# A down product set between the halves of the next expert's up product, expert weights read in longer runs, and a Hyena product taken last

## The chip, the cores and the metric

The kernel runs on one core of a Trainium2 chip (trn2). A core has a matrix engine (TensorE, PE in the profile; its weight loads are PEld), a vector engine (VectorE, DVE), an activation engine (ScalarE, ACT), GpSimd (POOL) and SyncE (SP), each with its own in-order queue, and 16 DMA engines that all queues share. The metric is the device time of one execution in microseconds; the time of record is the median of several runs.

## The reference, cut to what matters

The reference runs two blocks one after the other: a first block of two layers (an MLA attention layer and a Hyena layer with long convolutions), and a second block with sliding-window attention, an HGRN2 recurrence and a mixture of 32 experts with top-2 routing over 1024 tokens of width 1024. The change touches the projection of the Hyena layer and the experts:

```python
def hyena_seq(t, w_in, conv_w, conv_b, spec, bias, w_out):
    u, gate = jnp.split(t @ w_in, [(HY_ORDER + 1) * HY_WIDTH], axis=-1)   # t: 1024 x 1024, w_in: 1024 x 4096
    u = depthwise_conv(u, conv_w, conv_b)
    ...

    def expert_block(args):
        xb, e = args
        h = jax.nn.silu(xb @ w_gate[e]) * (xb @ w_up[e])   # w_gate, w_up: 1024 x 512
        return h @ w_down[e]                               # w_down: 512 x 1024
    y_blocks = lax.map(expert_block, (x_blocks, blk_e))
```

## The kernel before

Every large product is computed in a split form: each float32 operand is written as hi + lo (hilo, lines 162 to 165: ACT copies to hi, VectorE subtracts to get lo), and mm3 (lines 185 to 188) takes three matmuls, hi hi, hi lo and lo hi, into one PSUM tile. A planner (the tile scheduler, with a simulated timeline) lays down the order of each engine's instructions and gives out buffers when the program is built; the order of the statements is its priority.

**Hyena projection.** Lines 1015 to 1056 go over four column blocks c of 256 and, in each, over four chunks of the 4096 output columns: part 0 and part 1 (v and the first gate), the second gate, and the silu gate. Each chunk loads its weights (wchunk, lines 917 to 942) and projects (proj, lines 957 to 985); the first three also run a short convolution (convs and taps), and parts 0 and 1 are then transposed (line 1028). The projection is a fast matrix multiplication in the manner of Strassen and Winograd: seven products of half size in place of eight, on sums of weight blocks (s1 = x21 + x22, s2 = s1 - x11, s3 = x11 - x21, s4 = x12 - s2, made by GpSimd in total from two buffers in turn) and on sums of inputs (t1 to t4). Each product takes one PSUM bank out of a pool of five (ps3), is 12 matmuls of 512 columns and is then added into the result d by VectorE (add); the first, x11, is copied by ACT (line 971). In the chunks with a convolution d is a tile u, of which there are two for each chunk's two halves, so that a new chunk's first copy waits for the taps of the chunk before. The order of the products is x11, x12, s2, s3, s4, s1, x22. The weight tiles of each kind have one buffer (pool hywo), written by split for the next chunk when the product has read them. Only the first chunk has a hook, mid, and runs in two cuts of 256 columns.

**Experts.** Each of the 32 experts is a generator, expert (lines 1930 to 1992). It gathers up to 112 token rows by an indirect DMA on GpSimd's queue (xg), transposes them (line 1955) and splits them to xh and xl; then come the gate product (two weight tiles), the up product (two tiles), h = silu(gate) * up, the transposes of h (line 1977) with their split to hh and hl, the down product (two tiles, one for each half of the output columns), ACT's scaling to y (line 1989) and an accumulating indirect DMA of y to the output (line 1990). A weight tile is 1 MiB, [128, 4, 512]; load (lines 1935 to 1947) takes one of the raw buffers (slot_of: 11, later 8), issues one DMA on SP's queue and splits it into one of five hi and lo pairs. Of gate and up, partition p holds rows k * 128 + p, so that a tile has four runs of 2 KB in each partition; of down, a tile is 512 of 1024 columns of such rows, again runs of 2 KB. The driver (lines 2009 to 2014) steps through the generators with next: in iteration e it takes the gather of expert e+1, the first half of gate(e), the transposes of h(e-1), the second half of gate(e), down(e-1) and up(e). Two loads wait for marks (GATE, n = 9 and 10), and y comes from another pool when n has reached 62.

## Time and profile before

| | us |
|---|---|
| median of 3 runs | 3277.11 (3276.27 to 3277.31) |
| the profiled execution | 3279.27 |
| its span, first to last instruction | 3277.2 |
| TensorE busy in the span | 3089.8 (94%) |
| VectorE busy | 2467.8 (75%) |
| ACT busy | 1499.8 (46%) |
| GpSimd busy | 647.2 (20%) |
| mean granted TensorE clock | 0.979 |

Rows of the profile give times from the start of the span. A busy TensorE is not TensorE at its peak, since matmuls are pipelined and overlap; the spacing of their starts tells more than their durations. Idle time in brackets stands ahead of an instruction, with what ended it. The share of a DMA queue is the time of its packets as a share of 16 engines' time in the window.

### The profile page before, as it was taken

Reading aid. Unit: us, or ns where it says so; the run is one execution under the profiler, and the core shown is the slowest. Engines: PE = TensorE matmul, PEld = TensorE weight load, DVE = VectorE, ACT = ScalarE, POOL = GpSimd, SP = SyncE. Lnnn points to the kernel's source line nnn. Section 1 sums busy time; section 2 is a strip of 40 time slices with the busy share of each in tenths; the row PEclk is TensorE's granted clock in tenths of the full one; section 3 lists DMA queues with packets and bytes.
Section 4 is the critical chain, followed back from the end, with each engine's and each line's share of the span. In section 5 each row is a group of like instructions: output and inputs, shape, how many; then the busy total and the mean of one; then the engine's idle time right before and its main releaser. Section 6 shows DMA issues by size and latency. Waiting matters only on the chain. (4 is left out here: it accounts for less than half of the span.)

```text
span 3277.2 us, 49862 instructions
## 1 busy us (share of the span) xinstructions
PE 3089.8 (94%) x18178; PEld 2699.5 (82%) x18178; DVE 2467.8 (75%) x5292; ACT 1499.8 (46%) x2624; POOL 647.2 (20%) x523
## 2 busy tenths in 40 slices
PE   7899999999999899999999899999999989999997
PEld 3789888898987777889997799888878978777775
DVE  4985347888768888789897776576746689888886
ACT  2432234454543444421114345454523368777775
POOL 2651000000001434445750000000000024441110
PEclk9999999999999899999999999999999989999999
DMA  7562231331224222263426311312344689999996
GB/s 244 177 193 76 75 98 56 106 99 51 81 79 128 70 98 103 71 231 107 144 86 196 118 41 56 115 58 75 102 151 159 212 294 346 340 344 342 345 343 214
DMA packets 368879, 510.16 MB, mean 156 GB/s; under 512 B 59002, under 2 KB 211234, under 8 KB 368632
## 3 DMA queue, kind: packets, MB, share of 16 engines
q1 hardware_dynamic: 355464, 474.15, 43.8%
q0 software_dynamic: 13168, 32.81, 3.7%
q8 instruction: 144, 2.36, 0.3%
q14 instruction: 103, 0.84, 0.1%
HBM read 426.82 MB, written 92.61 MB: 158 GB/s over the span
## 5 line engine op out<-in xcount | busy, mean ns | idle before, releaser
L165 DVE TENSOR_TENSOR ewl<-ewr,ewh 128x1024 fp32r<-128x1024 f32 (+1 forms) x394 | 449.0, 1195 | 71.1 <-ACT ewh L164 70.1
L164 ACT ACTIVATE ewh<-ewr 128x1024 fp32r<-128x1024 f32 (+1 forms) x394 | 381.3, 1033 | 55.2 <-DMA ewr<-in_w_gate_experts_dram 20.4
L187 PE MATMUL ez<-ewl,xh 128*128 128x512 f32 x512 | 203.2, 397 | 5.9 <-DVE ewl L165 5.8
L186 PE MATMUL ez<-ewh,xh 128*128 128x512 f32 x512 | 201.3, 395 | 7.7 <-ACT ewh L164 7.7
L188 PE MATMUL ez<-ewh,xl 128*128 128x512 f32 x512 | 199.6, 390 | 0.0
L893 POOL TENSOR_TENSOR sd0h<-Yh,T 128x512 f32<-128x512 f32 x2 | 5.6, 2809 | 775.2 <-issue 769.9
L187 PE MATMUL cz<-cTl,w5h 128*128 128x512 f32 x384 | 152.7, 398 | 0.0
L186 PE MATMUL cz<-cTh,w5h 128*128 128x512 f32 x384 | 152.6, 399 | 0.0
L188 PE MATMUL cz<-cTh,w5l 128*128 128x512 f32 x384 | 152.1, 399 | 0.0
L164 ACT ACTIVATE pth<-tr 128x512 fp32r<-128x512 f32 x160 | 92.0, 594 | 130.1 <-PE tr L764 129.5
L747 DVE TENSOR_SCALAR_CACHE_REDUCE pr<-s 128x512 f32<-128x512 f32 (+1 forms) x192 | 109.2, 595 | 17.2 <-PE tr L764 11.2
L186 PEld LDWEIGHTS ez<-ewh,xh 128*128 128x128 f32 x512 | 96.4, 188 | 30.2 <-ACT ewh L164 10.4
L187 PEld LDWEIGHTS ez<-ewl,xh 128*128 128x128 f32 x512 | 96.4, 188 | 28.3 <-DVE ewl L165 9.1
L165 DVE TENSOR_TENSOR ptl<-tr,pth 128x512 fp32r<-128x512 f32 x160 | 107.4, 684 | 14.5 <-ACT pth L164 13.9
L186 PE MATMUL dz<-ewh,hh 128*128 128x512 f32 x256 | 101.2, 399 | 12.4 <-ACT hh L164 8.7
L188 PEld LDWEIGHTS ez<-ewh,xl 128*128 128x128 f32 x512 | 96.2, 188 | 19.0
L1990 POOL DMA_INDIRECT out_dram<-y,idx x32 | 75.6, 2364 | 170.9 <-ACT y L1989 129.7
L186 PE MATMUL oz<-owh,oh 128*128 128x512 f32 x256 | 102.4, 404 | 5.9 <-ACT owh L164 3.9
L751 ACT ACTIVATE pr<-pr,mx 128x1280 f32<-128x1280 f32 x64 | 87.3, 1364 | 41.1 <-DVE mx L750 40.6
L188 PE MATMUL oz<-owh,ol 128*128 128x512 f32 x256 | 100.8, 398 | 2.1 <-DVE ol L165 2.1
L187 PE MATMUL oz<-owl,oh 128*128 128x512 f32 x256 | 101.9, 399 | 0.0
L187 PE MATMUL dz<-ewl,hh 128*128 128x512 f32 x256 | 100.0, 391 | 0.2 <-DVE ewl L165 0.2
(758 smaller groups left out, 10827.1 us busy)
## 6 DMA issues: line engine op xcount, KB each, us to landing
ewr<-in_w_up_experts_dram SPq DMA_DIRECT2D x64, 1024.0 KB
ewr<-in_w_gate_experts_dram SPq DMA_DIRECT2D x64, 1024.0 KB
ewr<-in_w_down_experts_dram SPq DMA_DIRECT2D x64, 1024.0 KB
spec<-so SPq DMA_DIRECT2D x64, 256.0 KB
adaw<-in_ada_w_dram SPq DMA_DIRECT2D x64, 256.0 KB
hwr<-in_hy_w_in_dram SPq DMA_DIRECT2D x64, 256.0 KB
K<-spec SPq DMA_DIRECT2D x64, 256.0 KB
w5r<-in_w_in_dram SPq DMA_DIRECT2D x60, 256.0 KB
```

The lines of the kernel that those rows point to most:

```text
L164: S.activation(hi, x, AF.Copy)
L165: V.tensor_tensor(lo, x, rd(hi), ALU.subtract)
L186: T.matmul(ps, lh, rh, start=first, stop=False)
L187: T.matmul(ps, lh, rl, start=False, stop=False)
L188: return T.matmul(ps, ll, rh, start=False, stop=last)
L747: V.tensor_scalar(pr[:, k0:k0 + n], z[:, :n], 1.0, None, ALU.mult, ALU.max, accum_out=mx[:, c:c + 1])
L751: S.activation(pr, pr, AF.Exp, scale=SC, bias=mx[:, 3:4], accum_out=sm)
L893: G.tensor_tensor(t4, rd(yh[:, 4:, tk]), t2, ALU.subtract)
L1990: G.indirect_dma_start(out=out_d, out_offset=bass.IndirectOffsetOnAxis(ap=ix[:BR], axis=0), in_=y[:BR], in_offset=None, bounds_check=1023, ...
```

## The change

In proj, the s4 product moves from fifth to last place (in the cut that starts at column 256 it stays first, and in the first cut of the chunk with the hook it stays where it was). In expert, three things change. The weights are read so that partition p holds neighbouring rows, p * 8 + k for gate and up and p * 4 + k for down, and a tile is then one run of 8 KB in each partition; the transposes of xg and h read columns with a step of 8 and of 4 elements to match. A down tile is now two rows of all 1024 columns in each partition, so both output halves accumulate at once in two PSUM tiles over both weight tiles, and both loads stand ahead of the first matmul. The up product yields between its halves, and the driver takes one step more, so that iteration e is: gather of e+1, first half of gate(e), transposes of h(e-1), second half of gate(e), first half of up(e), down(e-1), second half of up(e).

```diff
--- before.py
+++ after.py
@@ -974,15 +974,15 @@
                 z22 = product("s4", "y22") if r.start else None
                 add(0, 1, (1, 0), product("s2", "t2"))
                 add(1, 1, (0, 1), product("s3", "t3"))
-                z22 = z22 or product("s4", "y22")
                 if mid and not r.start:
+                    z22 = product("s4", "y22")
                     with tc.issue_after(pe[0].ins):
                         mid()
                 z = product("s1", "t1")
                 add(1, 0, (1, 1), product("x22", "t4"))
                 add(1, 1, (1, 1), z)
                 add(0, 1, (0, 1), z)
-                add(0, 1, (0, 1), z22)
+                add(0, 1, (0, 1), z22 or product("s4", "y22"))
 
         def convs(wt, ct, mid=None):
 
@@ -1930,7 +1930,9 @@
     def expert(px, pw, praw, ps, pst, xg, ix, wt, e, static=True):
 
         def src(w):
-            return (w[e] if static else w[bass.ds(e, 1)].rearrange("o d f -> (o d) f")).rearrange("(k p) f -> p k f", p=P)
+
+            w = (w[e] if static else w[bass.ds(e, 1)].rearrange("o d f -> (o d) f")).rearrange("(p k) f -> p (k f)", p=P)
+            return w[:, :2048], w[:, 2048:]
 
         def load(w):
             n = n_raw[0]
@@ -1938,7 +1940,7 @@
             raw = slot_of(n).tile([P, 4, 512], F32, tag="ewr", name="ewr")
             if n in GATE:
                 V.tensor_copy(raw[:, 0, :1], GATE[n])
-            SY.dma_start(raw, w)
+            SY.dma_start(raw.rearrange("p k f -> p (k f)"), w)
             hi = pw[n % 5].tile([P, 4, 512], F32R, tag="ewh", name="ewh")
             lo = pw[n % 5].tile([P, 4, 512], F32R, tag="ewl", name="ewl")
             m = 1 if n < 5 else 2
@@ -1949,21 +1951,22 @@
                              bounds_check=1023, oob_is_err=False)
         xh = px.tile([P, 8, P], F32R, tag="xh", name="xh")
         xl = px.tile([P, 8, P], F32R, tag="xl", name="xl")
+        xk = xg.rearrange("t (p k) -> t k p", k=8)
         for k4 in range(2):
             z = pst.tile([P, 4, P], F32, tag="tr", name="tr")
             for k in range(4):
-                T.transpose(z[:, k], xg[:, (k4 * 4 + k) * P:(k4 * 4 + k + 1) * P], ident)
+                T.transpose(z[:, k], xk[:, k4 * 4 + k], ident)
             hilo(xh[:, k4 * 4:k4 * 4 + 4], xl[:, k4 * 4:k4 * 4 + 4], z)
         yield
         zz = []
         for w in (wg, wu):
             z = ps.tile([P, 512], F32, tag="mm", name="ez")
             for k4 in range(2):
-                wh, wl = load(src(w)[:, k4 * 4:k4 * 4 + 4])
+                wh, wl = load(src(w)[k4])
                 for k in range(4):
                     kk = k4 * 4 + k
                     mm3(z, xh[:, kk], xl[:, kk], wh[:, k], wl[:, k], kk == 0, kk == 7)
-                if w is wg:
+                if w is wg or k4 == 0:
                     yield
             zz.append(z)
         h = px.tile([P, 512], F32, tag="h", name="h", bufs=1)
@@ -1973,20 +1976,22 @@
         hh = px.tile([P, 4, P], F32R, tag="hh", name="hh", bufs=1)
         hl = px.tile([P, 4, P], F32R, tag="hl", name="hl", bufs=1)
         z = pst.tile([P, 4, P], F32, tag="tr", name="tr")
+        hk = h.rearrange("t (p k) -> t k p", k=4)
         for k in range(4):
-            T.transpose(z[:, k], h[:, k * P:(k + 1) * P], ident)
+            T.transpose(z[:, k], hk[:, k], ident)
         hilo(hh, hl, z)
         yield
         if n_raw[0] < 62:
             y = px.tile([P, 1024], F32, tag="y", name="y")
         else:
             y = praw[0].tile([P, 4, 512], F32, tag="ewr", name="y")[:, :2].rearrange("p a c -> p (a c)")
-        for c in range(2):
-            z = ps.tile([P, 512], F32, tag="mm", name="dz")
-            wh, wl = load(src(wd)[:, :, c * 512:(c + 1) * 512])
-            for k in range(4):
-                mm3(z, hh[:, k], hl[:, k], wh[:, k], wl[:, k], k == 0, k == 3)
-            S.activation(y[:BR, c * 512:(c + 1) * 512], z[:BR], AF.Copy, scale=wt[:BR])
+        zz = [ps.tile([P, 512], F32, tag="mm", name="dz") for _ in range(2)]
+        ws = [load(w) for w in src(wd)]
+        for c, k in ((0, 0), (1, 0), (0, 1), (1, 1), (0, 2), (0, 3), (1, 2), (1, 3)):
+            wh, wl = (x[:, k % 2 * 2 + c] for x in ws[k // 2])
+            mm3(zz[c], hh[:, k], hl[:, k], wh, wl, k == 0, k == 3)
+            if k == 3:
+                S.activation(y[:BR, c * 512:(c + 1) * 512], zz[c][:BR], AF.Copy, scale=wt[:BR])
         G.indirect_dma_start(out=out_d, out_offset=bass.IndirectOffsetOnAxis(ap=ix[:BR], axis=0), in_=y[:BR], in_offset=None,
                              bounds_check=1023, oob_is_err=False, compute_op=ALU.add)
         yield
@@ -2010,7 +2015,7 @@
     next(blocks[0])
     for e in range(33):
         cur, prev = [blocks[e]] if e < 32 else [], [blocks[e - 1]] if e else []
-        for b in blocks[e + 1:e + 2] + cur + prev + cur + (prev + cur if e < 31 else cur + prev):
+        for b in blocks[e + 1:e + 2] + cur + prev + cur + cur + (prev + cur if e < 31 else cur + prev):
             next(b)
         if 2 <= e < 18:
 
```

## Rows read from the trace of the kernel before

**Rows 1.** The page: busy time of TensorE, and DMA share in 40 slices

```profile
PE 3089.8 (94%) x18178; PEld 2699.5 (82%) x18178; DVE 2467.8 (75%) x5292; ACT 1499.8 (46%) x2624; POOL 647.2 (20%) x523
DMA  7562231331224222263426311312344689999996
```

**Rows 2.** Hyena chunks: stretch, us, busy PE PEld DVE ACT POOL, clock, DMA share, GB/s

```profile
1119.66:1144.88 25.22, 23.14 (x101) 18.64 (x100) 20.65 (x24) 11.60 (x22) 10.34 (x9) 0.93 0.35 125
1183.64:1205.01 21.37, 21.37 (x101) 17.73 (x100) 16.65 (x22) 10.17 (x21) 6.82 (x7) 1.00 0.15 49
1205.01:1233.27 28.26, 24.09 (x101) 19.29 (x100) 21.40 (x24) 11.93 (x23) 11.71 (x8) 0.88 0.31 112
...
1381.98:1410.45 28.47, 24.30 (x101) 19.50 (x100) 21.40 (x24) 12.04 (x23) 11.70 (x8) 0.88 0.06 19
```

**Rows 3.** Timeline of TensorE, 1216 to 1223: start, us, instruction [idle before, releaser]

```profile
1216.14 0.50 PE L186 MATMUL uz<-Y22h,s4h 128*128 128x512 f32 x1
...
1221.04 0.79 PE L188 MATMUL uz<-Y22h,s4l 128*128 128x512 f32 x1 [4.17 <-DVE s4l L165]
1221.64 0.63 PE L186 MATMUL uz<-Y22h,s4h 128*128 128x512 f32 x1
1222.06 0.63 PE L187 MATMUL uz<-Y22l,s4h 128*128 128x512 f32 x1
```

**Rows 4.** Timeline of ACT, the copy of line 971

```profile
1223.43 0.60 ACT L971 ACTIVATE u<-uz 128x512 f32<-128x512 f32 x1
```

**Rows 5.** Timeline of VectorE, 1202 to 1224

```profile
1202.40 0.69 DVE L165 TENSOR_TENSOR s1l<-ws,s1h 128x512 fp32r<-128x512 f32 x1 [2.37 <-ACT s1h L164]
1205.21 0.69 DVE L968 TENSOR_TENSOR u<-u,uz 128x512 f32<-128x512 f32 x1 [2.12 <-PE uz L188]
...
1207.96 1.27 DVE L968 TENSOR_TENSOR u<-u,uz 128x512 f32<-128x512 f32 x2
...
1220.31 0.68 DVE L165 TENSOR_TENSOR s4l<-ws,s4h 128x512 fp32r<-128x512 f32 x1
1220.91 2.43 DVE L1006 SCALAR_TENSOR_TENSOR y<-u,cw,y 128x512 f32<-128x512 f32 x2
```

**Rows 6.** The columns of rows 2, two stretches of the experts

```profile
2700.00:2800.00 100.00, 99.73 (x475) 82.68 (x475) 92.94 (x93) 84.76 (x103) 44.88 (x26) 1.00 1.02 347
2800.00:3250.00 450.00, 421.46 (x1944) 341.09 (x1943) 375.63 (x369) 341.70 (x413) 102.74 (x67) 1.00 0.99 338
```

**Rows 7.** Groups of TensorE, 2800 to 3250: busy, mean ns, idle before, releasers

```profile
L186 PE MATMUL ez<-ewh,xh 128*128 128x512 f32 x373 | 146.4, 393 | 7.7 <-ACT ewh L164 7.7
...
L186 PE MATMUL dz<-ewh,hh 128*128 128x512 f32 x187 | 73.9, 399 | 10.4 <-ACT hh L164 7.0 <-ACT ewh L164 3.3
```

**Rows 8.** DMA queues, 2800 to 3200: packets, MB, share of 16 engines

```profile
q1 hardware_dynamic: 63500, 126.11, 89.7%
```

**Rows 9.** The same, 3226 to 3231: expert tiles alone, runs of 2 KB

```profile
q1 hardware_dynamic: 973, 1.93, 104.4%
```

**Rows 10.** The same, 2578 to 2580: whole rows, runs of 4 KB

```profile
q1 hardware_dynamic: 222, 0.84, 102.4%
```

**Rows 11.** The same, 104 to 106: runs of 1 KB

```profile
q1 hardware_dynamic: 727, 0.71, 103.3%
```

**Rows 12.** Timeline of TensorE: transposes in Hyena, and in the experts

```profile
1197.56 1.61 PE L1028 MATMUL tr<-ident,y 128*128 128x128 f32 x12
1198.92 0.48 PE L186 MATMUL uz<-T1h,s1h 128*128 128x512 f32 x1
...
2740.13 0.60 PE L1955 MATMUL tr<-ident,xg 128*128 128x128 f32 x4
2740.49 0.48 PE L186 MATMUL ez<-ewh,xh 128*128 128x512 f32 x1
```

**Rows 13.** One line's instructions: ns min/median/max, first and last start

```profile
L1028 PEld LDWEIGHTS tr<-ident,y x128: 196/213/230, 1098.2 to 1408.8; 128*128 128x128 f32 x128
...
L1955 PEld LDWEIGHTS tr<-ident,xg x256: 137/141/231, 2648.1 to 3200.4; 128*128 128x128 f32 x128
```


## The prediction

> **What bounds the kernel now.** I read the page first. TensorE is busy for 94% of the span, so a microsecond is won only where TensorE stands, and the row of DMA shares is full in one place, the last fifth [rows 1]. Those are the two stages the diff touches. Next I read the busy time by stretch, once for single Hyena chunks (one call of proj: 84 matmuls of 512 columns and up to 16 transposes) and once for the expert stage.
>
> In Hyena an undisturbed chunk with 16 transposes takes 21.37 us with TensorE full. The chunk behind it takes 28.26 us for as many instructions at a granted clock of 0.88; two more of that kind follow, the last of 28.47, and a milder one before of 25.22 [rows 2]. The reader is to see 6.9 + 7.0 + 7.1 + 3.85 = 24.9 us beyond 21.37 (for the unshown one I take 7.0, between its neighbours). The timeline of TensorE shows the cause: the third matmul of the s4 product waits 4.17 us for s4l, and the next ones start 0.42 us apart, where (21.37 - 1.8 for the transposes)/84 = 0.23 is usual, so the wait is paid again in clock [rows 3].
>
> In the experts, TensorE is full (99.73 of 100 us) from 2700 to 2800 and executes 475 instructions; one expert is 72 matmuls and 12 transposes, 84, so 100/(475/84) = 17.7 us per expert. From 2800 to 3250 it is 1944 instructions, 23.1 experts, at 19.45 us each, with the DMA engines at 0.99 [rows 6]. The waits of TensorE there are small ones on ACT's ewh and hh [rows 7]; ACT is fed by the loads. This stretch is bound by the transfers, and if they cost nothing it would be (19.45 - 17.7) x 23.1 = 41 us shorter.
>
> **The change, part by part.**
>
> *Hyena order.* In 15 of 16 chunks s4 moves from fifth to seventh product (the cut with the hook mid keeps its order). Nothing is added. s1 and x22, 12 matmuls of 0.23 us each, come before it: s4 is due 5.5 us later, at about 1221.7 in the chunk shown, and s4l ends at 1220.31 + 0.68 = 1221.0 [rows 5]. So the wait on s4l goes. What is late next is a PSUM bank: the pool has five, x11, x12, s2, s3 and the fifth product fill them, and the sixth needs the bank of x11, which the copy of line 971 empties only at 1223.43 + 0.60 = 1224.0 [rows 4], behind the last tap of the chunk before (to 1223.34 [rows 5]). The sixth product was s1, hidden behind the s4l stall; now it is x22, ready to start at 1218.9. From below: if that copy stays at 1224.0, x22, s4 (2.75 us each) and 16 transposes (1.8) end at 1231.4 instead of 1233.27, a gain of 1.9 us, times three, and nothing in the milder chunk: 6 us in all. From above: 24.9. Which end is nearer is decided by VectorE. Before that backlog it idles 2.37 us for s1h (whose buffer waits for the s1 product of the chunk before, now 2.75 us earlier) and 2.12 us for the end of x22; then come four additions in a bunch, three of which (two for s1, one for x22) can now run in that idle time [rows 5]. That pulls the taps, hence the copy, forward by up to 4.5 us, to about 1219.5 to 1220, 1 us behind x22. I take 5.3 us for each of three and 2 for the milder: 18 us. Queues: no DMA moves; on VectorE the s1 and x22 additions go ahead of that of s4, and one instead of four follows the last product. s4's single weight buffer is written for the next chunk after its product, now 5.5 us later; that product is again a whole chunk away.
>
> *Expert loads.* Before, each partition of a 1 MiB tile comes in four runs of 2 KB; after, in one of 8 KB. Price of a run = share x 16 engines x time / runs. At 1 KB: 1.033 x 16 x 2 us / (0.71 MB/1024) = 47.7 ns [rows 11]; 2 KB: 1.044 x 16 x 5 / (1.93 MB/2048) = 88.6 ns [rows 9]; 4 KB: 1.024 x 16 x 2 / (0.84 MB/4096) = 159.8 ns [rows 10]. From 1 to 4 KB that is 37.4 ns per KB and 10.3 ns per run. No run of 8 KB is in the trace. Carried on along this line it is 310 ns (along 2 to 4 KB, 302), against 4 x 88.6 = 354; if a run is cut at 4 KB, 320; if only bytes count, no gain. Over 2800 to 3200 with gathers and scatters beside, a 2 KB run takes 0.897 x 16 x 400 / (126.11 MB/2048) = 93.2 ns [rows 8]. Per expert and engine there are 6 x 128 / 16 = 48 runs of 8 KB: 48 x (4 x 93.2) = 17.9 us now. Gain per expert: 0 at least (below it only if long runs hold the gathers up, which are issued an expert ahead), 48 x (373 - 302) = 3.4 us at most. I take what the line says for three runs less, 48 x 3 x 10.3 ns = 1.5 us, or 34 us over 23.1 experts. TensorE's own limit is as near (41 less 6 for the transposes below), and between two limits so close neither is reached: 30 us. *The Trainium skill* (DMA: Bandwidth & Descriptors, Why small descriptors are slow) gives an overhead of about 3 cycles per packet beside one per 32 bytes; by that, as an estimate, 2 KB to 8 KB saves 9 of 268 cycles, 0.6 us per expert and 14 us in all. The rows of this trace show more overhead than that.
>
> *Down inside up.* The 24 down matmuls of expert e-1 go from before up(e) to between its halves; their two loads on SP's queue go behind the first up load, and both stand ahead of the first down matmul; the scatter on POOL and y on ACT move with them. Between h and down(e-1) there are now 36 matmuls instead of 24, 2.7 us more for ACT's hh; the wait for hh there is 7.0 us [rows 7], and I count it within the 41, not again. Each tile still serves 12 matmuls, so the five hi/lo pairs turn as before. Two dz banks are open together, of five; two ez banks beside them leave one for the next gate. The gated loads n = 9 and 10 are the same tiles as before, and the tile y changes its pool at the same expert. Cost: nothing, while ACT is ready; if y0, now 6 matmuls later, holds ACT, that is 1.4 us per expert of an engine busy 342 of 450 us [rows 6].
>
> *Strided transposes.* xg is read with a step of 32 bytes and h of 16 bytes, where before columns were adjacent: 384 transposes. The nearest row is line 1028, with a step of 16 bytes: 12 in 1198.92 - 1197.56 = 1.36 us, 0.113 each, against 0.36 / 4 = 0.09 for the adjacent xg [rows 12]; +0.023 us or 9 us in all, 6 of them after 2800, where they only lower TensorE's limit to 41 - 6 = 35; so 2 us, those before 2800, count beside the 30. The upper bound is the whole difference of the weight loads, 213 - 141 = 72 ns [rows 13], 28 us; the lower one is nothing, since no row shows a step that loads faster. A rule against the change stands in the Trainium skill (SBUF — State Buffer, The DMA port swizzle, on cachelines): each access that crosses to a new 16-byte line pays. The rows agree in sign: 213 against 141 ns; a step of 32 bytes is shown by none.
>
> *Sum.* Hyena 18, experts 30 - 2 = 28: 46 us. The profiled execution took 3279.27 us with a span of 3277.2, 2.2 above the median of 3277.11; the sum is differences within the span, so 3277 - 46 = **3231**.
>
> **The rivals.**
> - *The stall only moves.* The bank of x11 comes no earlier and x22 waits where s4 did. For it: the copy at 1224.0 lies 5 us after x22 could start [rows 4]. Against it: VectorE's idle time before [rows 5]. Hyena 6: 3277 - 34 = 3243.
> - *Bytes bind, not runs*, or a run of 8 KB is split: the transfers don't gain, and the strided transposes cost 3. For it: the mean of 2800 to 3250 is 338 GB/s with the engines at 0.99 [rows 6]. Against it: 1.93 MB / 5 us = 386 and 0.84 MB / 2 us = 420 GB/s [rows 9, 10]. 3277 - 18 + 3 = 3262. A rule that would make it so is in the Trainium skill (HBM Reference, Specifications): about 358 GB/s effective per core. By that the stretch would be at its limit; the rows above it speak against that here, as does the page's own remark that a core alone measures more.
> - *The transposes cost more than all gains*, the slower side: the 32-byte step loads weights several times slower, in TensorE's order, where nothing hides it. Break-even is 48/384 = 0.125 us more per transpose, from 0.09 to 0.215; at 0.25 us each it is 3277 - 48 + 61 = 3290. For it: the 16-byte step already loads half as long again [rows 13]. Against it: its pace rose by only 0.023 us [rows 12].
> - *The change doesn't do what it says*: a planner lays down each engine's order, and it may already place down(e-1) between the halves of up(e). Then that part is worth nothing, which the sum assumes.
>
> **How the numbers follow.** Forecast 0.55 (own range 3214 to 3250), the stall moves 0.14, bytes bind 0.18, transposes 0.08, the order laid otherwise to no effect 0.05. The low end is the forecast with Hyena at 24.9 and the experts at 41: 3277 - 66 = 3211, rounded down; the high end is the case of bytes with Hyena at 10: 3270. Range 3210 to 3270. About 0.2%, 6.6 us, can be told from no change: faster 0.83 (all of the first two, most of bytes bind), same 0.08, slower 0.09.
>
> **What would show it.** Right: no chunk of 28 us, at most 1 to 2 us of waiting per bad chunk, now on the first matmul of x22 for ACT's copy; runs of 8 KB and some 310 to 350 ns each; 18 us per expert. Wrong: the same clock dips with another releaser; a mean rate still at 340 GB/s; transposes over 0.2 us apart; or VectorE, 93 of 100 us busy where TensorE is full [rows 6], ahead of TensorE as what the experts wait for.

## The result and the profile after

The changed kernel takes 3243.47 us (median of four runs, 3241.60 to 3247.82) against 3277.21 for the kernel before, in four runs on the same chip: a ratio of 0.9897, with a 95% interval of 0.9885 to 0.9908. The profiled execution took 3243.77 us with a span of 3242.0. Forecast were 46 us, measured are 34.

In the rows, uz is the PSUM tile of the Hyena projection, ez that of the gate and up products, dz that of the down product. The records of the two traces say where the 34 us lie. The last matmul of the Hyena projection (uz) starts at 1411.2 instead of 1429.6 us, 18.4 earlier. The first expert product (ez) starts at 2633.9 instead of 2651.0; of the 18.4 us, 17.1 have arrived there. From there to the start of the last down matmul (dz) it is 589.1 instead of 607.6 us, the expert stage in what follows: 18.5 less. The tail behind is 18.9 instead of 18.7. So Hyena gave what was forecast (18), and the experts 18.5 instead of 28.

The page of the changed kernel, answering to [rows 1], with its packets and the share of the hardware queue in the whole span:

```profile
PE 3078.4 (95%) x18178; PEld 2696.0 (83%) x18178; DVE 2476.3 (76%) x5292; ACT 1495.1 (46%) x2624; POOL 647.0 (20%) x523
DMA  7562231332124222263426312312344679999995
DMA packets 295151, 510.16 MB, mean 157 GB/s; under 512 B 59002, under 2 KB 211234, under 8 KB 270328
q1 hardware_dynamic: 281736, 474.15, 42.7%
```

The bytes are the same as before, and there are still nines in the last fifth: the transfers there are as busy as before, only for a shorter time.

The Hyena chunks of the changed kernel, in the columns of [rows 2]: the milder one, an undisturbed one, the first and the last of the three long ones.

```profile
1120.94:1143.73 22.79, 21.58 (x101) 17.65 (x100) 20.43 (x25) 9.30 (x20) 9.79 (x8) 1.00 0.36 130
1182.50:1203.86 21.36, 21.36 (x101) 17.72 (x100) 16.50 (x20) 9.48 (x19) 9.61 (x8) 1.00 0.16 52
1203.86:1226.51 22.65, 21.72 (x101) 17.88 (x100) 20.26 (x26) 9.83 (x18) 10.36 (x8) 1.00 0.36 128
...
1369.41:1392.05 22.64, 21.72 (x101) 17.88 (x100) 20.26 (x26) 9.84 (x18) 10.35 (x8) 1.00 0.00 1
```

28.26 us have become 22.65, and the clock is whole: where TensorE waited 4.17 us and then ran at 0.88, it now waits 0.93 and stays at 1.00. The four chunks together win 2.4 + 5.6 + 5.75 + 5.8 = 19.6 us; that 18.4 of them show at the end is because Hyena also began 2.25 us later in this trace (first projection product at 1059.0 against 1056.8) and its other chunks differ a little. What is left of the wait is in the timeline of TensorE in that chunk (start, us, instruction, idle before and its releaser), answering to [rows 3]:

```profile
1217.73 1.12 PE L1028 MATMUL tr<-ident,y 128*128 128x128 f32 x8
1219.78 0.73 PE L1028 MATMUL tr<-ident,y 128*128 128x128 f32 x4 [0.93 <-DVE y L1006]
1220.38 0.50 PE L186 MATMUL uz<-T4h,x22h 128*128 128x512 f32 x1
```

The copy of line 971 in the timeline of ACT, answering to [rows 4]:

```profile
1219.73 0.60 ACT L971 ACTIVATE u<-uz 128x512 f32<-128x512 f32 x1
```

The timeline of VectorE, answering to [rows 5]:

```profile
1198.46 0.69 DVE L165 TENSOR_TENSOR s1l<-ws,s1h 128x512 fp32r<-128x512 f32 x1 [2.64 <-ACT s1h L164]
1201.27 0.69 DVE L968 TENSOR_TENSOR u<-u,uz 128x512 f32<-128x512 f32 x1 [2.12 <-PE uz L188]
...
1216.01 0.68 DVE L165 TENSOR_TENSOR s4l<-ws,s4h 128x512 fp32r<-128x512 f32 x1
1217.87 1.76 DVE L1006 SCALAR_TENSOR_TENSOR y<-u,cw,y 128x512 f32<-128x512 f32 x1
```

TensorE waits before x22 as forecast (0.93 us), but its order has four transposes of y there, and their releaser is the last tap on VectorE (y, line 1006). x22 itself starts at 1220.38, just as the copy of line 971 ends (1219.73 + 0.60), so this trace doesn't tell the forecast's wait for the copy from the wait for the taps. The two idle times of VectorE, 2.64 and 2.12 us, are still there.

The experts of the changed kernel, in the columns of [rows 6]:

```profile
2700.00:2800.00 100.00, 100.00 (x476) 83.86 (x475) 88.76 (x89) 81.19 (x101) 45.61 (x27) 1.00 0.96 348
2800.00:3200.00 400.00, 388.85 (x1796) 316.95 (x1795) 349.64 (x345) 315.98 (x384) 83.48 (x60) 1.00 0.98 362
```

TensorE's groups of 2800 to 3200, answering to [rows 7]:

```profile
L186 PE MATMUL ez<-ewh,xh 128*128 128x512 f32 x343 | 134.0, 396 | 6.6 <-DVE h L1974 5.2 <-ACT h L1973 1.4
...
L186 PE MATMUL dz<-ewh,hh 128*128 128x512 f32 x174 | 59.2, 390 | 0.0
```

The hardware queue of 2800 to 3200, answering to [rows 8]:

```profile
q1 hardware_dynamic: 18460, 134.34, 87.1%
```

In the first stretch an expert takes 17.65 us, as before. In the second it is 1796 / 84 = 21.4 experts in 400 us, 18.7 each, where it had been 19.45. A run costs 0.871 x 16 x 400 us / (134.34 MB / 8192) = 340 ns; four short ones had cost 4 x 93.2 = 373. The waits for ACT's splits, before 7.7 us for ewh and 10.3 for hh and ewh ahead of dz [rows 7], are gone.

### The profile page after: what moved, and what is told of

Read it like the earlier page. It is cut to its first block, busy times and chain, and to the rows that moved or that the text cites. A ratio compares the mean times of both kernels' runs of the same rounds, so it can differ in the third digit from the quotient of the medians.

```text
span 3242.0 us, 49903 instructions
## 1 busy us (share of the span) xinstructions
PE 3078.4 (95%) x18178; PEld 2696.0 (83%) x18178; DVE 2476.3 (76%) x5292; ACT 1495.1 (46%) x2624; POOL 647.0 (20%) x523
## 5 line engine op out<-in xcount | busy, mean ns | idle before, releaser
L747 DVE TENSOR_SCALAR_CACHE_REDUCE pr<-s 128x512 f32<-128x512 f32 (+1 forms) x192 | 109.3, 595 | 17.7 <-PE tr L764 11.6
L1950 POOL DMA_INDIRECT xg<-hn_d,idx x32 | 50.0, 1561 | 294.5 <-PE tr L1958 287.5
L751 ACT ACTIVATE pr<-pr,mx 128x1280 f32<-128x1280 f32 x64 | 87.3, 1364 | 40.8 <-DVE mx L750 40.4
L164 ACT ACTIVATE yh<-yf 128x512 fp32r<-128x512 f32 x48 | 28.5, 626 | 157.5 <-POOL yf L1141 142.6
```

The lines of the kernel that those rows point to most:

```text
L164: S.activation(hi, x, AF.Copy)
L747: V.tensor_scalar(pr[:, k0:k0 + n], z[:, :n], 1.0, None, ALU.mult, ALU.max, accum_out=mx[:, c:c + 1])
L751: S.activation(pr, pr, AF.Exp, scale=SC, bias=mx[:, 3:4], accum_out=sm)
L1950: G.indirect_dma_start(out=xg[:BR], out_offset=None, in_=hn_d, in_offset=bass.IndirectOffsetOnAxis(ap=ix[:BR], axis=0), bounds_check=1023, ...
```

## The experiments

All kernels were compared with the kernel before on their own chip (median there 3277.66, 3280.92 and 3280.12 us for the three groups of four). The stretch from the last projection product to the first expert product, which no edit touches, took 1221.4 to 1231.0 us in the fourteen traces. A time alone is thus uncertain by some 5 us, and the stages are read from the traces. A stage has a spread too: in after, s4_sixth and x22_first, which have the same expert code, the expert stage took 589.1, 589.3 and 595.3 us. So the 18.5 us of the experts are known to some 6 us.

| kernel | time, us | ratio (95%) | last uz starts | expert stage |
|---|---|---|---|---|
| before | 3277.21 | | 1429.6 | 607.6 |
| after | 3243.47 | 0.9897 (0.9885 to 0.9908) | 1411.2 | 589.1 |
| hyena_only | 3267.64 | 0.9964 (0.9949 to 0.9979) | 1411.3 | 608.6 |
| runs_only | 3262.10 | 0.9952 (0.9936 to 0.9968) | 1412.1 | 608.9 |
| perm2k | 3268.91 | 0.9972 (0.9958 to 0.9987) | 1411.8 | 608.3 |
| place_only | 3289.47 | one run | 1429.1 | 612.5 |
| run4k | 3249.27 | 0.9919 (0.9904 to 0.9934) | 1409.4 | 590.5 |
| own_banks | 3246.52 | 0.9892 (0.9876 to 0.9909) | 1410.9 | 598.5 |
| five_loads | 3222.44 | 0.9821 (0.9804 to 0.9837) | 1411.7 | 569.3 |
| base_five | 3223.83 | one run | 1411.3 | 573.7 |
| runs_five | 3259.86 | one run | 1415.4 | 605.8 |
| place_five | 3219.38 | one run | 1410.3 | 569.5 |
| s4_sixth | 3259.38 | one run | 1418.7 | 589.3 |
| x22_first | 3255.47 | 0.9924 (0.9911 to 0.9938) | 1406.1 | 595.3 |

### Hyena: which order, and what it works on

**hyena_only** puts the new order alone into the kernel before.

```diff
-                z22 = z22 or product("s4", "y22")
                 if mid and not r.start:
+                    z22 = product("s4", "y22")
...
-                add(0, 1, (0, 1), z22)
+                add(0, 1, (0, 1), z22 or product("s4", "y22"))
```

> The kernel before with the new order of the Hyena products alone (s4 last in the second half of a chunk); the experts are as before. Theory (the two parts are independent): first expert product 17 to 18 us earlier, expert stage 607.5 us as before, time 3259.5, ratio 0.9946. Rival (the expert stage, bound by its loads, waits part of the gain away, so that it only pays together with the longer runs): first expert product still 17 us earlier, expert stage longer by 5 us or more, time 3265 to 3275. In both the disturbed chunks read 22.6 to 22.8 us and not 28.3.

The long chunks read 22.65 to 22.66 us and the last projection matmul starts at 1411.3, as in the changed kernel; the expert stage is 608.6 us, 1.0 longer. The gain of the order is its own, as far as the stage goes. Only 10 of the 18.4 us stood in the time, which is the rival's 3265 to 3275, but not for the rival's reason: the expert stage didn't lengthen by 5 us, the untouched stretch ahead of it did (1226.8 us here against 1221.4).

My theory at this point was that the stall had been the lateness of s4l. Two more orders test it. **s4_sixth** moves s4 back by one place only, **x22_first** keeps s4 last and moves x22 one place further forward.

```diff
 s4_sixth
                 z = product("s1", "t1")
+                z22 = z22 or product("s4", "y22")
                 add(1, 0, (1, 1), product("x22", "t4"))
...
-                add(0, 1, (0, 1), z22 or product("s4", "y22"))
+                add(0, 1, (0, 1), z22)
 x22_first
-                z = product("s1", "t1")
                 add(1, 0, (1, 1), product("x22", "t4"))
+                z = product("s1", "t1")
```

> The changed kernel with the Hyena products in the order s1, s4, x22 in the second half of a chunk, so that s4 moves back by one product and not by two. Theory A (the old stall was only the split of s4, which now ends at 1216.0 us in the chunk that starts at 1203.9): chunks of 22.6 to 23.5 us, last projection product within 8 us of 1411.2. Theory B (x22 stands ahead of s4 because the VectorE adds behind it release a bank and the tap chain of the next chunk one product earlier): chunks of 25 to 27 us, last projection product at 1420 to 1428 us.

> The changed kernel with the Hyena product x22 one place further forward: s3, x22, s1, s4 in the second half of a chunk, where the changed kernel has s3, s1, x22, s4. Theory (the chunk's stall is the chain of VectorE adds and taps that starts behind x22, so each place is worth up to one product of 2.8 us: 28.4, 25.5 and 22.65 us with x22 last with s4 ahead of all, last behind s4, and fifth): the 1.09 us that is left goes, chunks of 21.4 to 21.6 us instead of 22.65, last projection product 4 to 6 us earlier than 1411.2, time 3236 to 3240. Rival (what is left is the split of the longest weight sum or a bank): chunks of 22.6 us or more, time 3241 to 3248.

Three chunks of s4_sixth (columns as in [rows 2]):

```profile
1204.24:1228.29 24.05, 21.61 (x101) 17.63 (x100) 19.92 (x23) 11.07 (x21) 9.81 (x8) 1.00 0.36 131
1288.45:1314.01 25.56, 23.10 (x102) 19.03 (x100) 19.94 (x23) 11.17 (x21) 10.64 (x9) 0.93 0.34 124
1374.17:1399.57 25.40, 22.96 (x102) 18.95 (x100) 19.91 (x23) 11.17 (x21) 9.82 (x8) 0.93 0.00 1
```

Its timeline of TensorE ahead of s4, in the first of them:

```profile
1220.70 1.68 PE L1029 MATMUL tr<-ident,y 128*128 128x128 f32 x12 [2.44 <-DVE y L1007]
```

The same three chunks of x22_first:

```profile
1202.27:1223.62 21.35, 21.35 (x101) 17.73 (x100) 21.06 (x24) 9.29 (x19) 8.55 (x7) 1.00 0.42 148
1283.77:1305.46 21.69, 21.69 (x101) 17.57 (x100) 20.35 (x23) 8.76 (x19) 8.20 (x7) 1.00 0.42 147
1365.61:1386.96 21.35, 21.35 (x101) 17.73 (x100) 21.06 (x24) 9.18 (x19) 8.54 (x7) 1.00 0.08 25
```

The waits of TensorE from 1100 to 1412 us (us in total, times, longest), in the kernel before, in s4_sixth and in the changed kernel; x22_first has none on uz or y:

```profile
PE uz L188 <- DVE s4l L165: 14.6, 4, 4.2
PE tr L1029 <- DVE y L1007: 8.9, 5, 2.5
PE tr L1028 <- DVE y L1006: 4.0, 4, 1.2
```

In s4_sixth TensorE doesn't wait for s4l at all: it waits 2.44 us for y, the taps of the chunk before. The first step, from s4 fifth to s4 sixth with x22 last in both, is s4's own: the late chunks go from 28.3 to 28.5 us to 24.05 to 25.6, and TensorE waits for y instead, 1.7 us less. The next two move x22 forward: with x22 sixth the chunks take 22.65, with x22 fifth 21.35 to 21.7, which is TensorE full. The wait in such a chunk goes 4.17, 2.44, 0.93 and 0 us. The rest of each step is TensorE's own time at a lower granted clock: 24.1 to 24.3 us at 0.88, 23.0 to 23.1 at 0.93, 21.4 to 21.7 at 1.00. Once s4 is out of the way, what binds is the chain that starts at x22: the addition behind it, the taps of line 1006, the transposes and the copy of line 971 in the next chunk. Theory B of s4_sixth holds, with its chunks and its end a little earlier than it said.

x22_first ends this stage 5.1 us earlier, as its theory said, but its time is 3255 us and not 3236 to 3240: the stretch behind took 1231.0 us against 1222.7 in the changed kernel, and the expert stage, with the code of the changed kernel, 595.3 against 589.1. By 1820 us the 5 us are gone in its trace (the output products oz end at the same time in both kernels). So it is not shown to be better.

### Experts: each half of the change alone

**runs_only** is the changed kernel with the old driver order (8 KB runs, strides and down tiles by rows stay). **perm2k** is the changed kernel with the placement, rows and strides, but with every second 2 KB block of a partition in a tile, so that no run is longer than 2 KB; its down tiles are by half columns again. **place_only** is the kernel before with the placement alone.

```diff
 runs_only
-                if w is wg or k4 == 0:
+                if w is wg:
...
-        for b in blocks[e + 1:e + 2] + cur + prev + cur + cur + (prev + cur if e < 31 else cur + prev):
+        for b in blocks[e + 1:e + 2] + cur + prev + cur + (prev + cur if e < 31 else cur + prev):
 perm2k
-            return w[:, :2048], w[:, 2048:]
+            w = w.rearrange("p (k o f) -> p o k f", o=2, f=512)
+            return w[:, 0], w[:, 1]
...
-                    kk = k4 * 4 + k
+                    kk = k * 2 + k4
 place_only (on the kernel before)
-                if w is wg:
+                if w is wg or k4 == 0:
...
+        for b in blocks[e + 1:e + 2] + cur + prev + cur + cur + (prev + cur if e < 31 else cur + prev):
```

> The changed kernel without the placement: the down product of an expert again stands ahead of the whole up product of the next one; 8 KB runs, strided transposes, the half-tiles of the down weights with two banks, and the Hyena order stay. Theory A (the gain of the experts is that of the runs, the placement hides only the wait for hh and for the two banks, some 8.7 + 3.0 us of which the shorter transfers do not take away): time 3247 to 3256, the wait of dz for hh back at 5 us or more. Theory B (the placement costs as much as it hides, because the gate product now waits 0.9 us for the bank of the up product just before it): time 3238 to 3244. Theory C (the placement carries most of the expert gain): 3258 or more.

> The changed kernel with the same rows on the same partitions, strided transposes, placement, two banks and bytes, but each expert load takes every second 2 KB block of a partition's 16 KB, so no run is longer than 2 KB; the down weights come as one tile for each half of the columns again. Theory (the longer runs carry the experts' gain): packets of 88 to 92 ns for 2 KB, SDMA time 1.5 us an expert longer, expert stage 603 to 611 us instead of 589, time 3257 to 3266. Rival (bytes bind, the placement made the gain): packets dearer, but expert stage 589 to 593, time 3243 to 3247.

> The kernel before with the placement alone: the down product stands inside the next up product, loads of 2 KB runs, weight rows in the old order, unstrided transposes, down weights and banks by half columns, old Hyena order. Theory (short runs bind, as in the kernel with permuted 2 KB blocks: 608.3 us): expert stage 604 to 609 us, time 3273 to 3280. What it tells against that kernel is the price of rows and strides: strided transposes at 12 each an expert and 0.002 to 0.01 us more each would make 1 to 4 us, so 604 to 607 here; if they cost 0.02 us each as I had it at first, 600 us.

Expert stages: 608.9, 608.3 and 612.5 us, against 607.6 and 608.6 for the old stage. Neither half wins anything in the stage alone; together they win 18.5. Behind the stage runs_only is 5.7 us shorter than hyena_only (a tail of 14.7 against 20.3 us, one scatter of y being left there where hyena_only has two), which is about what their times differ by; their intervals overlap. For runs_only my theories A and B missed, and C, "the placement carries most", holds for its number only, for with short runs the placement carries nothing either. perm2k came out in the stage as its theory said and 3 us slower in time; place_only is 3.5 us above its theory in the stage and 9 in its one time. The same stretch, 2850 to 3150 us, in four kernels (columns as in [rows 6]), first the old stage (hyena_only):

```profile
2850.00:3150.00 300.00, 284.89 (x1305) 229.61 (x1304) 249.46 (x247) 228.01 (x275) 55.49 (x40) 0.99 1.02 347
```

runs_only:

```profile
2850.00:3150.00 300.00, 285.13 (x1308) 235.89 (x1307) 247.93 (x245) 226.98 (x277) 78.78 (x44) 0.98 0.98 351
```

perm2k:

```profile
2850.00:3150.00 300.00, 284.66 (x1277) 224.56 (x1276) 248.12 (x243) 225.74 (x272) 54.76 (x41) 0.99 1.01 346
```

The changed kernel:

```profile
2850.00:3150.00 300.00, 294.51 (x1364) 239.88 (x1363) 265.41 (x262) 240.38 (x293) 55.63 (x43) 1.00 1.00 367
```

With short runs the engines are full at 346 or 347 GB/s, placement or not. With long runs and the old order they are not full (0.98) and still deliver only 351; with both they deliver 367. So in runs_only something else holds TensorE back. The waits of TensorE for hh from 2640 to 3225 (us in total, times, longest), where the kernel before has 8.2 us:

```profile
PE dz L186 <- ACT hh L164: 23.8, 16, 3.4
```

One of its down products in the timeline of TensorE:

```profile
2866.44 0.63 PE L1981 MATMUL tr<-ident,h 128*128 128x128 f32 x4
2866.91 1.06 PE L1958 MATMUL tr<-ident,xg 128*128 128x128 f32 x8
2869.77 0.50 PE L186 MATMUL dz<-ewh,hh 128*128 128x512 f32 x1 [1.79 <-ACT hh L164]
```

And ACT at that time:

```profile
2861.56 7.68 ACT L164 ACTIVATE ewh<-ewr 128x1024 fp32r<-128x1024 f32 x8
2869.14 0.58 ACT L164 ACTIVATE hh<-tr 128x512 fp32r<-128x512 f32 x1
```

16 times dz stands still for hh, 23.8 us in all. hh is one of ACT's short operations, but here eight weight splits, 7.68 us, are ahead of it, so that it starts 2.06 us behind the last transpose of h; and between these transposes and dz no product is left to cover that time.

### Experts: the same forms with one load less

To separate TensorE's order from the transfers, four kernels take five loads of 1 MiB for each expert instead of six: the second down tile is split again from the first one's data, so that the products do the same work on other weights.

```diff
-        def load(w):
+        def load(w, old=None):
...
-            raw = slot_of(n).tile([P, 4, 512], F32, tag="ewr", name="ewr")
+            raw = old if old is not None else slot_of(n).tile([P, 4, 512], F32, tag="ewr", name="ewr")
...
-            SY.dma_start(raw.rearrange("p k f -> p (k f)"), w)
+            if old is None:
+                SY.dma_start(raw.rearrange("p k f -> p (k f)"), w)
+            raws[0] = raw
...
-        ws = [load(w) for w in src(wd)]
+        ws = [load(src(wd)[0]), load(None, raws[0])]
```

> The changed kernel with five weight loads of 1 MB for each expert instead of six: the second half of the down weights is split again from the first half's tile, so this part of the output is that of other weights; TensorE, ScalarE and VectorE do the same work. Theory B (transfers still bind in the last 350 us, where an expert takes 18.75 us against 17.5 to 17.75 us of TensorE work): expert stage 572 to 578 us, time 3226 to 3233. Theory A (only waits for banks and splits are left, transfers are hidden): expert stage 586 to 590 us, time 3240 to 3245.

> The expert stage before (2 KB runs, no placement; only the Hyena order is new), with five weight loads for each expert instead of six: the second down tile is split again from the first one's data, so this part of the output is that of other weights. Control of the next two. If a fifth less transfer is all that it takes, TensorE sets the time: expert stage 569 to 573 us, as the changed kernel with five loads (569.3). If the order itself makes TensorE wait for hh, 576 to 595.

> 8 KB runs without the placement, and five weight loads for each expert instead of six (the second down tile split again from the first one's data). With six loads this order had 23.8 us of waits of dz for hh, 16 of them. Theory (the waits for hh come from the order: hh is queued on ScalarE behind four weight splits of 3.9 us, and the placement hides that): waits for hh of 15 us or more stay, expert stage 584 to 595 us. Rival (they come from late transfers in front of those splits): they go with the fifth load, expert stage 569 to 574.

> Placement, row layout, strides and two banks with 2 KB runs (every second block), and five weight loads for each expert instead of six (the second down tile split again from the first one's data). Theory (with the placement only the transfers are left as a limit, 19.5 us an expert with six short loads, so some 16.3 with five, under the 17.6 of TensorE): expert stage 569 to 573 us, no waits for hh. Rival (strides, banks or order cost TensorE time of their own): 576 or more.

| expert stage, us | six loads | five loads |
|---|---|---|
| old order, 2 KB runs | 607.6, 608.6 | 573.7 |
| old order, 8 KB runs | 608.9 | 605.8 |
| placement, 2 KB runs | 608.3 | 569.5 |
| placement, 8 KB runs | 589.1, 589.3, 595.3 | 569.3 |

The stretch from 2850 to 3150 us of five_loads (columns as in [rows 6]):

```profile
2850.00:3150.00 300.00, 300.00 (x1421) 251.58 (x1420) 273.57 (x271) 248.83 (x305) 105.19 (x49) 1.00 0.93 326
```

The same of base_five, the old order with short runs:

```profile
2850.00:3150.00 300.00, 297.94 (x1403) 246.41 (x1402) 271.50 (x269) 247.34 (x302) 94.09 (x42) 1.00 0.98 324
```

The same of runs_five:

```profile
2850.00:3150.00 300.00, 283.87 (x1328) 236.98 (x1327) 256.11 (x254) 235.59 (x285) 105.04 (x43) 0.99 0.88 304
```

The one wait of TensorE that its expert stage shows (us in total, times, longest):

```profile
PE dz L186 <- ACT hh L164: 31.6, 18, 2.7
```

A place where it occurs, in the timeline of TensorE:

```profile
2901.82 0.63 PE L1983 MATMUL tr<-ident,h 128*128 128x128 f32 x4
2902.29 1.06 PE L1960 MATMUL tr<-ident,xg 128*128 128x128 f32 x8
2905.15 0.50 PE L186 MATMUL dz<-ewh,hh 128*128 128x512 f32 x1 [1.79 <-ACT hh L164]
```

With the placement TensorE is full, with either run length: 300 / 1421 x 84 = 17.7 us an expert. So with six loads the changed kernel is still bound by its transfers, by 589.1 - 569.3 = 20 us (20 to 26 over the traces with its expert code). five_loads and base_five came out 3 us below and 1 us above the ranges of the theories that they bear out, and runs_five 11 us above its own.

In the old order with long runs a load less helps by 3 us only; the wait for hh stays and even grows to 31.6 us, with the DMA engines at 0.88. So the transfers aren't what binds there. But it isn't the old order by itself either: with short runs and the old down tiles base_five reaches 573.7 us in that order, with 3.5 us of waits for hh. Nor does hh come later on ACT: behind the last transpose of h it starts 2.06 us in the median in runs_five and 2.04 in base_five. What differs is what the planner laid on TensorE in that time. Between the last transpose of h and the first dz the program has 12 products in both; laid are 0 in the median in runs_five (18 of 32 experts have none) and 12 in base_five. In the forms with the placement it is 18 to 24, and the wait for hh is 0.8 us at most. So the form that comes with the long runs brought this limit in, and the placement took it away. Why the planner leaves nothing between them there (down tiles by rows, which need both down loads ahead of the first dz, or its own estimate of times) was not separated and stays open: no run has long runs in the old order with the old down tiles.

### Experts: run length and banks

**run4k** has runs of 4 KB (pairs of rows of gate and up, single rows of down). **own_banks** gives the five banks out by hand, three in turn for gate and up, one for each half of down.

```diff
 run4k
-... .rearrange("(p k) f -> p (k f)", p=P)
-            return w[:, :2048], w[:, 2048:]
+... .rearrange("(g p k) f -> p g (k f)", p=P, k=k)
+            return w[:, :2], w[:, 2:]
 own_banks
-            z = ps.tile([P, 512], F32, tag="mm", name="ez")
+            z = ps.tile([P, 512], F32, tag=f"m{n_ez[0] % 3}", name="ez", bufs=1)
+            n_ez[0] += 1
...
-        zz = [ps.tile([P, 512], F32, tag="mm", name="dz") for _ in range(2)]
+        zz = [ps.tile([P, 512], F32, tag=f"d{c}", name="dz", bufs=1) for c in range(2)]
```

> The changed kernel with runs of 4 KB instead of 8 KB (gate and up in rows of pairs, down in single rows; the transposes then step by 8 bytes for xg and by 4 for h). By the run law of the traces (37.4 ns for each KB and 10.3 ns for each run) a load is 320 ns for 8 KB instead of 310, 0.4 us an expert over 24 loads of 128 KB... worked out as 24 x 1024 / 128 / 16 = 96 pieces of 8 KB for each engine of an expert, so 96 x 10.3 ns = 1.0 us less saved at most, and of the 589 us only what the transfers bind. Theory (transfers no longer bind after the change): time 3243 to 3247. Rival (transfers still bind in the last 350 us): 6 to 15 us longer, time 3249 to 3258. Third (the 32-byte step of the transposes cost something): up to 3 us shorter, 3240 to 3243.

(The count of 96 pieces in that text is wrong; it is 48 for an expert and engine, so the law gives 0.5 us.)

> The changed kernel with the five PSUM banks of the experts handed out by hand: three in turn for the gate and up products, one for each half of the down product. The pool of five had often put the gate product of the next expert into the bank of the up product just ended, and the gate product then waited 0.85 to 1.03 us for h (5.2 + 2.1 us in all after 2580 us). Theory A (these waits are lost time): they go, expert stage 580 to 584 us instead of 589.1, time 3235 to 3240. Theory B (the transfers bind after 2850 us, at 365 to 368 GB/s and a DMA share of 0.99 to 1.00, and would make TensorE wait elsewhere): the waits turn into waits for ewh or ewl of the same size, expert stage 588 to 592, time 3241 to 3247.

run4k: 590.5 us, 1.4 longer, and 365 GB/s in the stretch from 2850 to 3150. Packet times of the expert loads in the records: four of 2 KB 4 x 84 = 336 ns in the median and 4 x 92.8 = 371 in the mean, two of 4 KB 318 and 348, one of 8 KB 309 and 341. The difference between 4 and 8 KB, 7 ns x 48 = 0.3 us an expert, is too small for the stage to tell apart from its spread. The time of 3249.27 us is at the edge of the rival's range, which five_loads bears out in kind: the transfers still bind.

own_banks: the waits of ez for h are gone, and others stand in their place (TensorE, 2640 to 3225):

```profile
PE ez L186 <- ACT ewh L164: 6.5, 5, 2.6
PE ez L187 <- DVE ewl L165: 6.5, 12, 1.4
PE dz L186 <- ACT y L1995: 3.2, 2, 2.6
```

That is theory B in kind: most of it is waits for weights that arrive late (the 3.2 us on y are a new wait for a bank that the fixed assignment brings), and the stage is no shorter. It is 598.5 us in the profiled execution, the slowest of the four, where B said 588 to 592; the time is that of the changed kernel within its interval. So the bank wait was a place where TensorE stood while the transfers caught up, and no gain of its own is to be had from it here.

## Why the prediction was right, and where not

**Which stages, and the total.** The two stages named are the two that moved, and the time lies in the range of 3210 to 3270. It lies 12 us above the forecast and on the number of a rival, 3243 for "the stall only moves", by coincidence: Hyena gave its full 18 us, and the experts fell short.

**Hyena order: right in size, wrong in one reason.** 18 forecast, 18.4 measured; "5.3 us for each of three and 2 for the milder" measured 5.6 to 5.8 and 2.4. The wait left is 0.93 us at x22, "1 us behind x22". But I let the additions move into VectorE's idle time of 2.37 and 2.12 us [rows 5], and that idle time is still there. What moved is where the chain starts: x22 is no longer the last product, so that its addition and the taps behind it come one product earlier relative to the next chunk, and the copy of line 971 comes 15.9 us after the start of its chunk, not 18.4. The first addition behind the idle time lies 0.2 us behind the chunk's start before and 2.6 ahead of it after. The orders show it: with s4 out of the way and x22 last 2.44 us of wait stay, with x22 one place earlier 0.93, with two none. That the forecast for each chunk was met with this reason wrong is in part luck.

**Run prices: right.** 310 ns forecast for 8 KB ("302 to 310"), 309 in the median; packet time saved for an expert 48 x (373 - 340) = 1.6 us, forecast 1.5. The rule of the Trainium skill (DMA: Bandwidth & Descriptors, Why small descriptors are slow) gave, as an estimate, 9 of 268 cycles, 3.4%; measured, 336 to 309 ns is 8%.

**Expert loads: the mis-sized term.** I took 1.5 us x 23.1 = 34 and, next to TensorE's limit of 35, set 30. Measured are 0.75 us an expert (19.45 to 18.7) and 18.5 in all. Two steps failed. First, packet time is not stage time. Of the 1.6 us, 0.4 went into how full the engines are: between 2850 and 3150 the sum of all packet times is 1.015 of the window before and 0.996 after, 2% of 19 us, while gathers and scatters cost the same 2.2 us an expert in both. And the pace of the loads is not yet that of TensorE; the hardware queue in that stretch, before and after:

```profile
q1 hardware_dynamic: 47964, 95.27, 90.2%
q1 hardware_dynamic: 13937, 101.49, 87.6%
```

An expert is 6.29 MB, so its loads came every 19.8 us before and every 18.6 after, 1.2 us less. TensorE took 19.2 and 18.5 us an expert there (1315 and 1364 instructions, 84 each): the old kernel meanwhile used up tiles that had been loaded ahead, and so lost less to slow loads than I priced. Second, the limit I thought near, TensorE's, was not reached: at 18.7 an expert is a full microsecond above its 17.7, and the kernels with five loads show that this is still the transfers.

**Down inside up: "cost: nothing", and counted at nothing, was wrong the other way.** I counted 24 products between h and the down product before and 36 after. hh can only start behind the transposes of h, and from there the program has 12 and 24; laid are 12 and 24 in the median, but before in 8 of 32 experts none. More important, I counted the wait for hh "within the 41, not again", as if shorter transfers took it away. They don't: with long runs in the old order it grows from 8.2 to 23.8 us (2640 to 3225), and eats the whole gain of the stage. The placement is worth about 20 us behind long runs, where it covers this wait, and nothing behind short ones, where the transfers bind. In the rival "doesn't do what it says" I had written that the sum assumes it to be worth nothing; that assumption hid that the other part depends on it. That the long runs alone come out at just the old 608 us is a coincidence of two limits, the old one of the transfers and a new one for hh; base_five (573.7 us) shows that the old kernel did not have the second.

**PSUM banks.** "Two ez banks beside them leave one for the next gate" was the right place to look: 6.6 us of waits for h. By own_banks no time is won without them while transfers bind.

**Strided transposes: over-priced.** 9 us forecast, of which 2 in the sum and 6 off TensorE's limit; nothing measurable. Weight loads are indeed longer, 191 ns (xg, 32 bytes) and 210 (h, 16 bytes) in the median against 141 [rows 13]; the weight loads of these two lines in the changed kernel (ns min, median, max; first and last start):

```profile
L1958 PEld LDWEIGHTS tr<-ident,xg x256: 186/191/231, 2631.0 to 3161.7; 128*128 128x128 f32 x128
...
L1981 PEld LDWEIGHTS tr<-ident,h x128: 196/210/220, 2652.7 to 3216.6; 128*128 128x128 f32 x128
```

Their pace didn't change: eight of xg in a row take 0.101 us each (0.106 before), four 0.091 (0.089). I had compared line 1028, 12 in a row, with four of xg in a row, and the pace differs with their number: of the adjacent xg, four take 0.089 us each and eight 0.106. The slower rival is excluded by these paces. The rule of the Trainium skill on cachelines (SBUF — State Buffer, The DMA port swizzle) has its sign in the loads and none in the time.

**Bytes bind, not runs: excluded.** 345 GB/s before and 367 after in the same stretch, and 346 in perm2k with the same placement and rows as after, but short runs. The figure of 358 GB/s (the Trainium skill, HBM Reference, Specifications) is no limit here.

**What would show it.** "No chunk of 28 us", "runs of 310 to 350 ns", "no mean rate of 340" held; "18 us per expert" did not (18.7).

## What to carry to other kernels

An edit can bring in a limit of its own that hides what it saves: the long runs saved packet time and lost it to waits for hh, until the placement, which wins nothing without them, covered these. So price two edits of one loop together, and ask of a wait that seems to be covered by the bound whether it has a cause of its own. Count the cover of a short operation from where it can start, expert by expert in the laid order of the trace and not only in that of the program, and look at what its engine has queued ahead of it. To find which limit is left, remove one transfer and look whether the engine fills up.

## What the runs showed of the hardware that was not expected

- Removing one load of six took 34 us from the old stage (607.6 and 608.6 to 573.7), but 3 us from the form with long runs and the old order (608.9 to 605.8).
- A weight load a third longer (191 against 141 ns) cost TensorE nothing in a row of transposes: 0.101 us each for eight, strided, against 0.106 unstrided.
- The sum of packet times can exceed the window (1.02 of it with 2 KB runs), and 8 KB runs move 6% more bytes at 1.00 (367 against 347 GB/s). A share near 1 therefore says neither at which rate the DMA engines run nor that they bind: place_five reads 0.98 with TensorE busy for 300 of 300 us, and runs_only 0.98 with TensorE waiting for hh.
- A Hyena wait of 4.17 us also cost clock: the granted clock of the chunk was 0.88. Of three chunks with a wait of 2.4 to 2.5 us one read 1.00 and two 0.93, and those with a wait of 0.93 us read 1.00.
